# Feed-forward operand places queued by hand, GLA state in pairs, norms behind the last sums

## The chip, the cores and the metric

One core of one Trainium2 chip. The metric is device microseconds of one execution of the whole program, the median of several runs. TensorE is PE, VectorE DVE, ScalarE ACT, GpSimd POOL, and SP is the queue that issues the transfers.

## What is computed

One decoder layer, x of 1024 tokens by 1024 columns, float32. The parts that the change touches:

```python
# gated linear attention, per chunk of tokens (scan over chunks, 4 heads, 64 x 128 state a head)
def step(state, xs):
    qn, kn, vn, dn = xs
    o = jnp.einsum('bhid,bhde->bhie', qn, state)
    state = state * dn[..., None] + jnp.einsum('bhjd,bhje->bhde', kn, vn)
    return state, o
...
# feed-forward
h = rmsnorm(x, pre_ffn_g[l])
gt = causal_dwconv(h @ w_ff_gate[l], ff_conv_w[l]) + ff_conv_b[l]
y = (jax.nn.gelu(gt, approximate=True) * (h @ w_ff_up[l])) @ w_ff_down[l]
x = x + rmsnorm(y, post_ffn_g[l])
```

Besides these the layer has the input projection, a short convolution, dilated attention, gates and an output projection.

## The kernel before

**Products.** A float32 matrix is split into a high and a low part (`split`, L155 to L159: ACT copies the high part, L158, and DVE subtracts it, L159), and each product is three matmuls, high by high, high by low, low by high. Dense products are done two by two blocks at a time with seven products instead of eight. `seven` (L265 to L320) takes 256 columns of a weight: it loads two raw halves (L169, 512 KB each), splits the operands 0, 1, 5, 6 from them, lets POOL form the combined ones (L279, L281, L283, L285), and issues the products 0 to 5, of 12 matmuls of 128x512 each (L292 to L295), with sums between them:

- L302 (ACT) and L304 (DVE): the first block of the result, from the banks X (product 0) and Y (1);
- L307 (ACT): from Z, product 2;
- L310 (ACT) and L313 (DVE): from X, product 3, and from Z, product 4;
- L315 (DVE): from X, product 5.

Product 6 is put off: `last_product` issues it behind product 0 of the next `seven`. It goes on in the bank X of its own block, so it has to wait for L315 of that block. Operands 0 to 3 lie in one slot of the pool `wp` and 4 to 6 in the other; a slot is free again when the last product that reads it has ended.

**Feed-forward, first stage** (L1320 to L1365). Ten chunks of 256 columns follow one done beforehand. Each has a `seven` on the gate's weight (a gate block), whose results go through the convolution (`conv`, L1270 to L1284: ACT L1278, DVE L1279, L1280, L1282, L1283, ACT L1284), and one on the up weight (an up block), whose results are multiplied on (L1342). `forms` (L1291 to L1307) then stores the result's blocks to DRAM and lets POOL make four combined ones (`made`, L1295), stored as well (`keep`, L1287), in the order 5, 7, 6, 3. The first of them overwrites a22 and so waits for a22's store.

**Feed-forward, second stage** (L1443 to L1497). Again seven products, in the order 2, 1, 5, 6, 3, 7, 4, each over 11 chunks, in four groups of matmuls of 128x512 (L1469), with sums L1475 to L1484. The operands of a step are loaded, combined and split some steps ahead. The table `ENDS` says behind which step the norm of which tile comes: `h` is `finish_half` (squares L1423, multiplication L1425) and `f` is `finish` (the reciprocal root and L1440). Product 7's sums (L1484) were issued with high priority.

**GLA state loop** (L797 to L826). Eight chunks of 128 tokens. For each head one product of the chunk itself (L805, 128 deep) and one with the state (L807, 64 deep: two heads share the partitions) add up in one place of a bank; the next state's update is a product with 64 columns of weights per head (L812), and DVE scales and adds (L817). Results leave by ACT (L823) and DVE (L826). Matmuls of the branch projection (`p`, L198 to L202) are put between the chunks by the scheduler, and behind the loop follow a norm (L836), POOL's L838 and transposes (L842).

Where no order is written out, a scheduler sets each engine's queue; every engine works off its own in order.

## Time and profile before

| what | us |
|---|---|
| median of 3 runs | 1990.79 |
| lowest, highest | 1985.05, 1993.75 |
| the profiled execution | 1983.94 |
| its span | 1982.1 |
| PE, DVE, ACT, POOL busy | 1897.9, 1302.5, 875.7, 756.7 |

The granted clock of PE is 0.987 of full speed in the mean. A row of a timeline gives start, duration, engine, line, operation and tiles; matmuls are pipelined, so a row's duration is longer than the distance from one start to the next. The GLA state loop lies at 937 to 975 us of the span, the feed-forward's first stage at 1360 to 1758, its second behind it.

### The profile page before, as it was taken

How to read it: one execution, taken by the hardware profiler on the slowest of the kernel's cores; microseconds unless marked ns; L12 is line 12 of the kernel's file. 1: busy time of each engine (PE TensorE's matmuls, PEld its weight loads, DVE VectorE, ACT ScalarE, POOL GpSimd, SP SyncE). 2: the span in 40 equal slices, each digit the busy share in tenths (PEclk: the TensorE clock that was granted, in tenths of full speed). 3: DMA queues.
4: the chain of work that ended last, by engine and by line, in shares of the span. 5: the costliest groups of instructions: out<-in, count | busy, mean ns of one | idle time of the engine just before them, and what ended most of it. 6: DMA issues, size and time to landing. Idle time of an engine off the chain costs nothing.

```text
span 1982.1 us, 26264 instructions
## 1 busy us (share of the span) xinstructions
PE 1897.9 (96%) x9705; PEld 1601.8 (81%) x9705; DVE 1302.5 (66%) x1913; ACT 875.7 (44%) x1618; POOL 756.7 (38%) x457
## 2 busy tenths in 40 slices
PE   6999999999999999999999898998999999999997
PEld 5988778888787999899688776886888788878885
DVE  8755665677777332578545577577667766678595
ACT  5343345454444323435356623343434443454543
POOL 4522334554555221102214463016444444516172
PEclk9999999999999999999999998999999999999998
DMA  4121323232323424113467554221323233378752
GB/s 174 64 91 59 122 85 122 92 126 91 122 96 126 135 75 146 59 38 102 137 194 218 168 173 157 85 101 54 106 87 127 80 107 105 108 279 319 264 179 101
DMA packets 187072, 251.53 MB, mean 127 GB/s; under 512 B 30017, under 2 KB 121023, under 8 KB 186944
## 3 DMA queue, kind: packets, MB, share of 16 engines
q1 hardware_dynamic: 186944, 249.86, 37.5%
q8 instruction: 76, 1.25, 0.2%
q14 instruction: 52, 0.43, 0.1%
HBM read 183.34 MB, written 66.47 MB: 126 GB/s over the span
## 4 chain that ended last, share of the span: by engine, by line
PE 64%; DVE 18%; issue 5%; POOL 4%; ACT 4%; DMA 4%; SPq 0%; DVEq 0%; POOLq 0%; ACTq 0%
PE sX L295 19%; PE sZ L295 8%; DVE wl L159 6%; PE sY L295 5%; PE fY L1469 4%; PE fX L1469 4%; PE vX L567 3%; PE vZ L567 2%; PE mx L1229 1%; PE mx L1230 1%; PE mx L1228 1%; PE gs L749 1%; ACT wh L158 1%; PE p L198 1%; PE p L200 1%
## 5 line engine op out<-in xcount | busy, mean ns | idle before, releaser
L159 DVE TENSOR_TENSOR wl<-raw,wh 128x512 fp32r<-128x512 f32 (+1 forms) x214 | 216.1, 1043 | 119.7 <-ACT wh L158 116.7
L295 PE MATMUL sX<-T,wh 128*128 128x512 f32 x720 | 224.3, 393 | 10.5 <-DVE ring L315 9.8
L158 ACT ACTIVATE wh<-raw 128x512 fp32r<-128x512 f32 (+1 forms) x226 | 146.1, 670 | 78.6 <-PE sX L295 59.6
L295 PEld LDWEIGHTS sX<-T,wh 128*128 128x128 f32 x720 | 134.8, 189 | 42.8 <-DVE ring L315 14.0
L295 PE MATMUL sX<-FT,wh 128*128 128x512 f32 x480 | 149.3, 392 | 9.1 <-DVE ring L315 6.8
L295 PE MATMUL sX<-T,wl 128*128 128x512 f32 x360 | 140.7, 391 | 0.0
L506 POOL TENSOR_TENSOR fr<-fr 128x512 f32<-128x512 f32 x48 | 71.8, 1496 | 144.0 <-ACT fr L499 142.6
L295 PEld LDWEIGHTS sX<-FT,wh 128*128 128x128 f32 x480 | 89.2, 188 | 32.2 <-DVE ring L315 11.5
L159 DVE TENSOR_TENSOR wl<-fr,wh 128x512 fp32r<-128x512 f32 x90 | 67.7, 773 | 64.8 <-ACT wh L158 64.1
L158 ACT ACTIVATE wh<-fr 128x512 fp32r<-128x512 f32 (+1 forms) x97 | 61.8, 657 | 77.0 <-PE sX L295 48.4
L295 PE MATMUL sX<-FT,wl 128*128 128x512 f32 x240 | 93.5, 389 | 0.0
L1295 POOL TENSOR_TENSOR fb<-fb 128x512 f32<-128x512 f32 x40 | 56.9, 1423 | 91.6 <-DMA d_fa<-fb 89.9
L279 POOL TENSOR_TENSOR fr<-raw 128x512 f32<-128x512 f32 x30 | 40.8, 1360 | 122.2 <-DMA raw<-in_w_gate_dram 45.7
L159 DVE TENSOR_TENSOR ops<-rw,ops 128x512 fp32r<-128x512 f32 x72 | 64.6, 927 | 28.4 <-ACT ops L158 28.2
L295 PEld LDWEIGHTS sX<-T,wl 128*128 128x128 f32 x360 | 68.0, 189 | 14.5
L285 POOL TENSOR_TENSOR raw<-raw 128x512 f32<-128x512 f32 x50 | 79.5, 1590 | 0.0
L507 DVE TENSOR_TENSOR ring<-ring,fr 128x512 f32<-128x512 f32 x48 | 57.2, 1193 | 30.8 <-POOL fr L506 29.3
L295 PE MATMUL sZ<-T,wh 128*128 128x512 f32 x240 | 73.9, 389 | 0.0
L1469 PE MATMUL fX<-ops 128*128 128x512 f32 x312 | 73.8, 391 | 0.0
L302 ACT ACTIVATE ring<-sX 128x512 f32<-128x512 f32 x48 | 28.5, 594 | 95.9 <-PE sX L295 75.2
L1469 PEld LDWEIGHTS fX<-ops 128*128 128x128 f32 x312 | 59.0, 189 | 12.3
L283 POOL TENSOR_TENSOR fr<-raw,fr 128x512 f32<-128x512 f32 x30 | 49.8, 1661 | 46.4 <-DVE wl L159 46.4
(552 smaller groups left out, 5623.2 us busy)
## 6 DMA issues: line engine op xcount, KB each, us to landing
rw<-in_w_ff_down_dram SPq DMA_DIRECT2D x99, 256.0 KB
raw<-in_w_in_dram SPq DMA_DIRECT2D x48, 512.0 KB
rw<-d_fa SPq DMA_DIRECT2D x77, 256.0 KB
d_fa<-fb SPq DMA_DIRECT2D x70, 256.0 KB
raw<-in_w_gate_dram SPq DMA_DIRECT2D x24, 512.0 KB
d_sig<-ring SPq DMA_DIRECT2D x48, 256.0 KB
d_qk<-ring SPq DMA_DIRECT2D x48, 256.0 KB
raw<-in_w_ff_gate_dram SPq DMA_DIRECT2D x22, 512.0 KB
```

The source lines that it names most:

```text
L158: S.activation(h, src, AF.Copy)
L159: eng.tensor_tensor(l, src, h.bitcast(F32), op=OP.subtract)
L279: G.tensor_tensor(s1, A21, A22, op=OP.add)
L283: G.tensor_tensor(s1, A12, s2, op=OP.subtract)
L285: G.tensor_tensor(A21, A11, A21, op=OP.subtract)
L295: PE.matmul(ps, a[x][:, k], b[y][:, k], start=first and k == 0 and n == 0, stop=k == 3 and n == 2, skip_group_check=not first)
L302: S.activation(c11, X, AF.Copy)
L506: G.tensor_tensor(sw, sw, sin[:, hs], op=OP.mult)
L507: V.tensor_tensor(as_(o), as_(o), perm(sw), op=OP.add)
L567: PE.matmul(o, b[y][:, k, ts], a[:, x, k], start=first and t % 2 == 0 and k == 0 and n == 0, stop=k == 3 and n == 2, skip_group_check=not ...
L1295: G.tensor_tensor(o, p, q, op=op)
L1469: PE.matmul(P[t], o[:, a, ts], o[:, b], start=st, stop=c + k == NCH - 1 and x == 2, skip_group_check=i not in (2, 1, 5))
```

## The change

- In the feed-forward's first stage a block's seven operands take seven of eight single places in turn, instead of two slots. Their splits are issued behind given sums of the block before (`issue_after`): operands 0 and 1 behind sums 2 and 1, operands 2 and 3 behind sums 3 and 4, the others behind 3 and 5, on ACT and DVE. Other uses of `seven` stay as they were.
- `forms` makes its four in the order 7, 5, 6, 3, with 7 written over a11.
- The GLA state holds two heads side by side, 256 columns, with zeros where they don't meet. A state product is one of 128 deep and 256 columns for two heads, and so is the update; the update's scaling on DVE is four instructions of 64x128 instead of two of 128x128.
- In the second stage the norms come later (`ENDS`); what they issue on DVE once product 7's sums are out is queued behind the last of these, and the high priority is gone.

```diff
--- before.py
+++ after.py
@@ -270,21 +270,33 @@
         r0, r1 = wload([v[:, :4, c0:c0 + 256], v[:, 4:, c0:c0 + 256]], [8, 256])
         A11, A21, A12, A22 = r0[:, :, :128], r0[:, :, 128:], r1[:, :, :128], r1[:, :, 128:]
         s1, s2 = [t.rearrange("p (k c) -> p k c", k=4) for t in tmp]
-        sets = []
-        for i in range(2):
-            sets.append([wp.tile([128, 4, 4, 128], F32R, name=n, tag=n) for n in ("wh", "wl")])
-        op = lambda i: (sets[i // 4][0][:, i % 4], sets[i // 4][1][:, i % 4])
-        split(*op(0), A11)
-        split(*op(1), A12)
+        if sops:
+            ops = [sops[0]() for i in range(7)]
+        else:
+            sets = [[wp.tile([128, 4, 4, 128], F32R, name=n, tag=n) for n in ("wh", "wl")] for i in range(2)]
+            ops = [(sets[i // 4][0][:, i % 4], sets[i // 4][1][:, i % 4]) for i in range(7)]
+        op = lambda i: ops[i]
+
+        def made(i, src):
+            with ExitStack() as es:
+                if sops:
+
+                    for k in ((2, 1) if i < 2 else (3, 4) if i < 4 else (3, 5)):
+                        if k in sums_taken:
+                            es.enter_context(tc.issue_after(sums_taken[k].ins))
+                split(*op(i), src)
+
+        made(0, A11)
+        made(1, A12)
         G.tensor_tensor(s1, A21, A22, op=OP.add)
-        split(*op(2), s1)
+        made(2, s1)
         G.tensor_tensor(s2, s1, A11, op=OP.subtract)
-        split(*op(3), s2)
+        made(3, s2)
         G.tensor_tensor(s1, A12, s2, op=OP.subtract)
-        split(*op(4), s1)
+        made(4, s1)
         G.tensor_tensor(A21, A11, A21, op=OP.subtract)
-        split(*op(5), A21)
-        split(*op(6), A22)
+        made(5, A21)
+        made(6, A22)
 
         blk = lambda j, l: (B[l][0][:, 4 * j:4 * j + 4], B[l][1][:, 4 * j:4 * j + 4])
         tt = lambda i: (Ts[i][:, 0], Ts[i][:, 1])
@@ -301,18 +313,18 @@
         c11 = dst(0, 0)
         S.activation(c11, X, AF.Copy)
         prod(Y, op(1), blk(1, 0), True)
-        V.tensor_tensor(c11, c11, Y, op=OP.add)
+        sums_taken[1] = V.tensor_tensor(c11, c11, Y, op=OP.add)
         prod(Z, op(2), tt(0), True)
         c22 = dst(1, 1)
-        S.activation(c22, Z, AF.Copy)
+        sums_taken[2] = S.activation(c22, Z, AF.Copy)
         prod(X, op(3), tt(1), False)
         c12 = dst(0, 1)
-        S.activation(c12, X, AF.Copy)
+        sums_taken[3] = S.activation(c12, X, AF.Copy)
         use(0, 0, c11)
         prod(Z, op(4), blk(1, 1), False)
-        V.tensor_tensor(c12, c12, Z, op=OP.add)
+        sums_taken[4] = V.tensor_tensor(c12, c12, Z, op=OP.add)
         prod(X, op(5), tt(2), False)
-        V.tensor_tensor(c22, c22, X, op=OP.add)
+        sums_taken[5] = V.tensor_tensor(c22, c22, X, op=OP.add)
         use(0, 1, c12)
         use(1, 1, c22)
 
@@ -323,6 +335,13 @@
 
 
     pending = []
+
+    sops, sums_taken = [], {}
+
+    def op_places():
+
+        ts = [[wp.tile([128, 4, 4, 128], F32R, name=n, tag=n) for n in ("wh", "wl")] for i in range(2)]
+        return Ring([(h[:, i], l[:, i]) for h, l in ts for i in range(4)])
 
     def last_product():
         while pending:
@@ -795,35 +814,40 @@
                              PQ[:, 2 + a, (2 * bp + bb) * 128:(2 * bp + bb) * 128 + 128], ident)
         ins = S.activation(kin[:, 2 * bp:2 * bp + 2], p.rearrange("p (b c) -> p b c", c=256), AF.Copy)
     ssg = sm.tile([128, 32], F32, name="ssg", bufs=1)
+
+
     state = None
-    states = slot("t2", [128, 2, 2, 128], name="states")
+    states = slot("t2", [128, 2, 2, 256], name="states")
+    G.memset(states, 0.0)
     for b in range(8):
-        po = [pt(tag, "go")[:, :256].rearrange("p (a e) -> p a e", a=2) for tag in "ot"]
-        for h in range(4):
-            bs = slice((h % 2) * 64, (h % 2) * 64 + 64)
-            p = po[h % 2][:, h // 2]
-            PE.matmul(p, Sb[:, b, h], gv[:, b, h * 128:h * 128 + 128], start=True, stop=b == 0)
+        po = [pt(tag, "go")[:, :256] for tag in "ot"]
+        for a in range(2):
             if b:
-                PE.matmul(p, qk[bs, h // 2, b * 128:b * 128 + 128], state[bs, h // 2], start=False, stop=True)
+                PE.matmul(po[a], qk[:, a, b * 128:b * 128 + 128], state[:, a], start=True, stop=True)
+            for w in range(2):
+                h = 2 * a + w
+                PE.matmul(po[a][:, w * 128:w * 128 + 128], Sb[:, b, h], gv[:, b, h * 128:h * 128 + 128],
+                          start=not b and w == 0, stop=True, skip_group_check=b > 0 or w == 1)
         if b < 7:
-            p2 = pt("s", "gst")[:, :256].rearrange("p (a e) -> p a e", a=2)
-            for h in range(4):
-                bs = slice((h % 2) * 64, (h % 2) * 64 + 64)
-                PE.matmul(p2[bs, h // 2], kin[:, b, h * 64:h * 64 + 64], gv[:, b, h * 128:h * 128 + 128],
-                          start=True, stop=True)
+            p2 = pt("s", "gst").rearrange("p (a e) -> p a e", a=2)
+            for a in range(2):
+                PE.matmul(p2[:, a], kin[:, b, a * 128:a * 128 + 128], gv[:, b, a * 256:a * 256 + 256],
+                          start=a == 0, stop=True, skip_group_check=a == 1)
             new = states[:, b % 2]
             for a in range(2):
-                if b:
-                    V.scalar_tensor_tensor(new[:, a], state[:, a], dec[:, a, b:b + 1], p2[:, a],
-                                           op0=OP.mult, op1=OP.add)
-                else:
-                    V.tensor_copy(new[:, a], p2[:, a])
+                for w in range(2):
+                    bs, es = slice(w * 64, w * 64 + 64), slice(w * 128, w * 128 + 128)
+                    if b:
+                        V.scalar_tensor_tensor(new[bs, a, es], state[bs, a, es], dec[bs, a, b:b + 1], p2[bs, a, es],
+                                               op0=OP.mult, op1=OP.add)
+                    else:
+                        V.tensor_copy(new[bs, a, es], p2[bs, a, es])
             state = new
         for h in range(4):
-            S.activation(gv[:, b, h * 128:h * 128 + 128], po[h % 2][:, h // 2], AF.Square,
+            S.activation(gv[:, b, h * 128:h * 128 + 128], po[h // 2][:, h % 2 * 128:h % 2 * 128 + 128], AF.Square,
                          accum_out=ssg[:, 4 * b + h:4 * b + h + 1])
-        for w in range(2):
-            V.tensor_copy(gv[:, b].rearrange("p (a w e) -> p a w e", w=2, e=128)[:, :, w], po[w])
+        for a in range(2):
+            V.tensor_copy(gv[:, b, a * 256:a * 256 + 256], po[a])
     rg = rstd(ssg, 128, 32)
 
 
@@ -1301,10 +1325,10 @@
             keep(c, 4, a22)
         if il == (1, 0):
             keep(c, 2, a12)
-            made(5, a22, a21, a22, OP.add)
-            made(7, a21, a11, a21)
-            made(6, a11, a22, a11)
-            made(3, a12, a12, a11)
+            made(7, a11, a11, a21)
+            made(5, a21, a21, a22, OP.add)
+            made(6, a22, a22, a11)
+            made(3, a12, a12, a22)
 
 
     first = [wcols(w_fg2, 0), wcols(w_fu2, 0)]
@@ -1325,6 +1349,8 @@
     for il in ((0, 0), (1, 1), (1, 0)):
         forms(0, ys, il)
 
+    sops.append(op_places())
+    sums_taken.clear()
     ring = halves_ring(("t2", "t0", "t1"))
     yring = Ring([fb[:, i] for i in (0, 1, 3)])
     STMP = [fb[:, 2, :512], fb[:, 2, 512:]]
@@ -1444,7 +1470,8 @@
 
     ALONE = {5 * NCH + 8: 3, 6 * NCH: 3, 6 * NCH + 6: 5}
 
-    ENDS = {(7, 1): "h0", (7, 3): "f0 h1", (7, 5): "f1 h2", (7, 7): "h3", (4, 3): "f2 h4 h5", (4, 4): "f3 h6", (4, 5): "h7"}
+    ENDS = {(7, 1): "h0", (7, 4): "f0", (4, 0): "h1 h2", (4, 3): "f1 h3 f2 h4", (4, 4): "f3 h5 h6", (4, 5): "h7"}
+    taken = None
     ready = []
     X = [pt("g", "fX") for t in range(4)]
     Y = [pt(tag, "fY") for tag in ("s", "s", "t", "o")]
@@ -1480,19 +1507,19 @@
                 elif i == 3:
                     V.tensor_tensor(C12[:, t], C12[:, t], P[t], op=OP.add)
                 elif i == 7:
-                    with tc.high_priority():
-                        V.tensor_tensor(C22[:, t], C22[:, t], P[t], op=OP.add)
+                    taken = V.tensor_tensor(C22[:, t], C22[:, t], P[t], op=OP.add)
                 else:
                     finish_half(4 + t, P[t], 0)
                     finish(4 + t)
-        for what in ENDS.get((i, c), "").split():
-            t = int(what[1])
-            if what[0] == "h":
-                if t < 4:
-                    finish_half(t, C11[:, t], 0)
-                finish_half(t, (C12, C22)[t // 4][:, t % 4], 1)
-            else:
-                finish(t)
+        with tc.issue_after(taken.ins) if taken else nullcontext():
+            for what in ENDS.get((i, c), "").split():
+                t = int(what[1])
+                if what[0] == "h":
+                    if t < 4:
+                        finish_half(t, C11[:, t], 0)
+                    finish_half(t, (C12, C22)[t // 4][:, t % 4], 1)
+                else:
+                    finish(t)
         n += w
```

DVE's queue in a gate block; L304, L313 and L315 are the sums, `wl` the low parts of operands, `fb` and `raw` their sources. Before:

```order
L304 TENSOR_TENSOR ring<-ring,sY 128x512
L1279 SCALAR_TENSOR_TENSOR fb<-ring,cols,fb 128x511
L1280 SCALAR_TENSOR_TENSOR fb<-ring,cols,fb 128x510
L159 TENSOR_TENSOR wl<-raw,wh 128x512 x2
L159 TENSOR_TENSOR wl<-fb,wh 128x512 x2
L313 TENSOR_TENSOR ring<-ring,sZ 128x512
L1279 SCALAR_TENSOR_TENSOR fb<-ring,cols,fb 128x511
L1282 SCALAR_TENSOR_TENSOR fb<-ring,cols,fb 128x1
L315 TENSOR_TENSOR ring<-ring,sX 128x512
L1280 SCALAR_TENSOR_TENSOR fb<-ring,cols,fb 128x510
```

and in the changed kernel, where the lines are 12 (sums) or 24 (convolution) further down, L316, L325 and L327 being the sums:

```order
L316 TENSOR_TENSOR ring<-ring,sY 128x512
L1303 SCALAR_TENSOR_TENSOR fb<-ring,cols,fb 128x511
L1304 SCALAR_TENSOR_TENSOR fb<-ring,cols,fb 128x510
L159 TENSOR_TENSOR wl<-raw,wh 128x512 x2
L325 TENSOR_TENSOR ring<-ring,sZ 128x512
L159 TENSOR_TENSOR wl<-fb,wh 128x512 x2
L1303 SCALAR_TENSOR_TENSOR fb<-ring,cols,fb 128x511
L1306 SCALAR_TENSOR_TENSOR fb<-ring,cols,fb 128x1
L1304 SCALAR_TENSOR_TENSOR fb<-ring,cols,fb 128x510
L327 TENSOR_TENSOR ring<-ring,sX 128x512
L1307 SCALAR_TENSOR_TENSOR fb<-ring,cols,fb 128x2
```

Two splits have moved behind the sum of product 4, and the sum of product 5 has moved behind one more instruction of the convolution.

DVE's queue up to product 7's sums (L1484) in the second stage, with the numbers of the buffers; `rr`, `rt` and `ro` belong to norms. Before:

```order
L151 TENSOR_SCALAR rt_14914<-rt_14914 128x1
L153 TENSOR_TENSOR ro_14917<-rr_14912,rt_14914 128x1
L1440 SCALAR_TENSOR_TENSOR acc_13392<-acc_13392,ro_14917,x1r_13394 128x512 x2
L159 TENSOR_TENSOR ops_13382<-rw_13380,ops_13382 128x512
L159 TENSOR_TENSOR ops_13382<-bs_13389,ops_13382 128x512
L159 TENSOR_TENSOR ops_13383<-rw_13380,ops_13383 128x512
L159 TENSOR_TENSOR ops_13383<-bs_13389,ops_13383 128x512
L1484 TENSOR_TENSOR acc_13393<-acc_13393,fX_13396 128x512
```

and in the changed kernel, where these sums are L1510:

```order
L159 TENSOR_TENSOR ops_13293<-rw_13291,ops_13293 128x512
L159 TENSOR_TENSOR ops_13293<-bs_13300,ops_13293 128x512
L159 TENSOR_TENSOR ops_13294<-rw_13291,ops_13294 128x512
L159 TENSOR_TENSOR ops_13294<-bs_13300,ops_13294 128x512
L1510 TENSOR_TENSOR acc_13304<-acc_13304,fX_13307 128x512
L1510 TENSOR_TENSOR acc_13304<-acc_13304,fX_13308 128x512
```

The norms have gone from between the splits; only splits stand ahead of the first of these sums.

PE's queue at one chunk of the GLA loop. Before (L812 the state's update, `p` the other matmuls):

```order
L812 MATMUL gst_7388<-gv_6095,gqk_6004 64x128 x3
L202 MATMUL p11_7576<-yH1h_7212,wh_7231 128x512
L198 MATMUL p10_7609<-yH1h_7212,wl_7232 128x512
L812 MATMUL gst_7411<-gv_6095,gqk_6004 64x128
L805 MATMUL go_7355<-gv_6095,Sb_6098 128x128
L807 MATMUL go_7355<-states_7266,gqk_6004 128x128
L805 MATMUL go_7356<-gv_6095,Sb_6098 128x128
L807 MATMUL go_7356<-states_7266,gqk_6004 128x128
```

and in the changed kernel (L826 the state products, L829 the chunk's own, L834 the update):

```order
L834 MATMUL gst_7358<-gv_6095,gqk_6004 128x256 x2
L826 MATMUL go_7329<-states_7266,gqk_6004 128x256
L829 MATMUL go_7329<-gv_6095,Sb_6098 128x128 x2
L826 MATMUL go_7330<-states_7266,gqk_6004 128x256
L829 MATMUL go_7330<-gv_6095,Sb_6098 128x128 x2
L834 MATMUL gst_7379<-gv_6095,gqk_6004 128x256 x2
```

Four state products have become two, the update's four two, and no `p` stands between.

## Rows read from the trace of the kernel before

**Rows 1.** The page, part 1: engine, busy us (share of the span), instructions.
```profile
PE 1897.9 (96%) x9705; PEld 1601.8 (81%) x9705; DVE 1302.5 (66%) x1913; ACT 875.7 (44%) x1618; POOL 756.7 (38%) x457
```

**Rows 2.** Waits, PE, 1360 to 1760: us in total, times, longest.
```profile
PE sX L295 <- DVE ring L315: 6.8, 11, 1.7
...
PE sX L295 <- ACT ring L310: 2.3, 1, 2.3
```

**Rows 3.** Timeline, PE, a gate block: start, duration, instruction, [idle before, releaser].
```profile
1457.24 0.62 PE L295 MATMUL sX<-FT,wh 128*128 128x512 f32 x2
...
1462.46 0.39 PE L295 MATMUL sX<-F0h,wl 128*128 128x512 f32 x1
1464.06 0.73 PE L295 MATMUL sX<-FT,wh 128*128 128x512 f32 x2 [1.21 <-DVE ring L315]
```

**Rows 4.** Timeline, DVE, the same gate block.
```profile
1458.76 2.37 DVE L159 TENSOR_TENSOR wl<-fb,wh 128x512 fp32r<-128x512 f32 x2
1461.06 0.67 DVE L313 TENSOR_TENSOR ring<-ring,sZ 128x512 f32<-128x512 f32 x1
1462.53 0.75 DVE L1279 SCALAR_TENSOR_TENSOR fb<-ring,cols,fb 128x511 f32<-128x511 f32 x1 [0.79 <-ACT fb L1278]
...
1463.32 0.68 DVE L315 TENSOR_TENSOR ring<-ring,sX 128x512 f32<-128x512 f32 x1
```

**Rows 5.** Chain of waits, 1440 to 1480: start, duration, what.
```profile
1451.30 4.30 DMA raw<-in_w_ff_gate_dram
...
1464.06 3.02 PE sX L295 x12
```

**Rows 6.** Timeline, PE, one chunk of the GLA state loop.
```profile
953.72 0.49 PE L805 MATMUL go<-gv,Sb 128*128 128x128 f32 x2
954.13 0.48 PE L807 MATMUL go<-states,gqk 64*128 64x128 f32 x2
```

**Rows 7.** Chain of waits, 925 to 994.
```profile
937.55 0.89 PE go L805 x8
...
952.40 0.59 PE gst L812 x8
```

**Rows 8.** Stretches: us, PE, PEld, DVE, ACT, POOL busy, PEclk, DMA, GB/s.
```profile
1900.00:1942.00 42.00, 36.29 (x161) 29.71 (x159) 41.64 (x62) 19.73 (x43) 25.27 (x16) 0.99 0.51 176
1942.00:1948.00 6.00, 5.95 (x14) 4.72 (x15) 5.07 (x7) 5.90 (x14) 3.77 (x3) 0.50 0.05 22
1942.00:1982.00 40.00, 32.93 (x132) 26.71 (x132) 20.07 (x44) 12.98 (x31) 10.07 (x7) 0.88 0.15 56
```

**Rows 9.** Timeline, PE, end stage.
```profile
1942.05 1.62 PE L1469 MATMUL fX<-wh 128*128 128x512 f32 x3 [5.76 <-DVE acc L1484]
```

**Rows 10.** Timeline, DVE, end stage.
```profile
1928.85 0.75 DVE L1440 SCALAR_TENSOR_TENSOR acc<-acc,ro,x1r 128x512 f32<-128x512 f32 x1
...
1930.72 1.78 DVE L1440 SCALAR_TENSOR_TENSOR acc<-acc,ro,x1r 128x512 f32<-128x512 f32 x1
...
1934.18 1.41 DVE L1440 SCALAR_TENSOR_TENSOR acc<-acc,ro,x1r 128x512 f32<-128x512 f32 x2
...
1937.49 1.42 DVE L1440 SCALAR_TENSOR_TENSOR acc<-acc,ro,x1r 128x512 f32<-128x512 f32 x2
...
1941.23 1.88 DVE L1484 TENSOR_TENSOR acc<-acc,fX 128x512 f32<-128x512 f32 x3
```

**Rows 11.** Line L921: duration ns min/median/max, first and last start, forms.
```profile
L921 PE MATMUL ds<-dA x128: 270/379/615, 997.2 to 1121.7; 128*128 128x256 f32 x88, 128*128 128x128 f32 x40
```

**Rows 12.** Groups of instructions, 925 to 976: busy us, mean ns, idle before.
```profile
L826 DVE COPY gv<-go 128x256 f32<-128x256 f32 x15 | 6.0, 421 | 6.8 <-ACT gv L823 6.8
...
L817 DVE SCALAR_TENSOR_TENSOR states<-states,dec,gst 128x128 f32<-128x128 f32 x12 | 4.1, 345 | 13.9 <-PE go L807 11.4 <-PE gst L812 2.5
```

**Rows 13.** Timeline, PE, behind the GLA loop.
```profile
984.39 0.66 PE L842 MATMUL yT<-cst,sg 128*128 128x128 f32 x4 [1.01 <-POOL sg L838]
```

**Rows 14.** Tile raw, 1400 to 1700: duration ns min/median/max.
```profile
L159 DVE TENSOR_TENSOR wl<-raw,wh x60: 677/693/1776, 1409.3 to 1690.1; 128x512 fp32r<-128x512 f32 x60
```

## The prediction

> **What bounds the kernel now.** I read the page first: TensorE (PE) is busy 96% of the span [rows 1]. So a change pays only where PE stands still or where its own instructions get cheaper, and PE's waits by stage, the timelines and the chain have to say where. Three places are touched.
>
> In the feed-forward's first stage PE waits 11 times, 6.8 us in all, for the sum L315 on VectorE (DVE), and once 2.3 us for the copy L310 on ScalarE (ACT) [rows 2]. One gate block shows the first kind. Product 5 starts at 1457.24; with the next block's product 0 behind it, 24 matmuls, 0.227 us apart, it reaches to 1462.7. The deferred seventh product needs product 5's bank and starts only at 1464.06, after 1.21 us idle [rows 3]. DVE's rows say why: L313, which needs only product 4 (done when product 5 starts), begins at 1461.06, since splits stand ahead of it, two of them of 2.37 us together; L1279 then waits for ACT, and L315 begins at 1463.32 [rows 4]. Twelve matmuls after such a restart take 3.02 us [rows 5] instead of 12 x 0.227 = 2.72.
>
> In the GLA state loop PE never stops; the price of an instruction is the limit. An intra-chunk product (128 rows deep) and a state product (64 rows deep) alternate, two instructions each, and a pair of instructions starts 0.41 us after the one before: 0.21 an instruction [rows 6]. Eight intra-chunk ones on end, in chunk 0, take 0.89, so 0.11 each; eight of the state update, with weights of 64 columns, 0.59, so 0.07 [rows 7].
>
> Before the last product of the end stage DVE is the bound: busy 41.64 of the 42 us up to 1942 [rows 8]. PE waits 5.76 us, up to 1942.05, for the sums L1484 [rows 9], the first of which starts at 1941.23 [rows 10]. From 1942 to 1948 the granted clock is 0.50, the lower of its two levels (1.2 GHz) [rows 8].
>
> **The change part by part.** *Operand places and forms.* A block's operands 2 and 3 get places of their own, so their splits needn't stand ahead of L313; in a gate block they are queued behind it, and L315 now behind both L1279 and L1280. Counted from the block's start (six products of 2.72 before 1457.24): product 4 ends at 16.3, L313 starts at 16.4 to 17.1 (a raw split may still run) and takes 0.67, mostly in the shadow of the next start; the two splits take 2.37; from L1279's start to L315's are 0.79 now, to which L1280 adds 0.75 at most; L315 takes 0.68 [rows 4]. With L313 at its full 0.67 that ends between 21.7 and 22.4; rows that follow each other start up to 0.1 before the last has ended, five times here, so 21.2 to 21.9. PE needs it at 16.32 + 2 x 2.72 = 21.76. I leave 0.1 us of stall per chunk. The present loss: 6.8 less the last block's 1.7, which has no gate block behind it, is 5.1 [rows 2], and ten slow restarts of 0.3 make 3.0; of 8.1, 1.0 stays. On GpSimd (POOL) the forms now begin with one that doesn't wait for a store, stores follow earlier, and I let the first block's L310 wait 0.4 instead of 2.3: 1.9 more. Of the 9.0 I take **8**, as a late L310 also puts off the first L315. Ends: 10, and 1.9 where the gates gain nothing. No instruction is added; but on ACT both raw splits now stand ahead of L310, and on SP the weight loads lie between the stores 7, 5, 6, 3 (rival (d)).
>
> *GLA.* Before, a chunk with state: eight pairs at 0.41 to 0.42, 3.3 us, and the update 0.59 for eight: over seven chunks 27.4 [rows 6, 7]. After: 8 intra-chunk instructions at 0.11, and 4 of the state and 4 of the update with 256 columns. The nearest row for those is L921: 88 of its 128 matmuls have 256 columns and the median lasts 379 ns, the shortest, of 128 columns, 270 [rows 11]; 0.11 more than 0.11 is 0.22. So 0.89 + 0.88 + 0.88 = 2.65 us, 18.5 over seven: 9 us less. The memset on POOL is over before the loop. But hardly any other matmul now stands between the chunks, so what DVE needs must fit: four updates of 345 ns and two copies of 421 make 2.2 us [rows 12]. 0.4 is to spare, and I give back 0.3 a chunk: **7**. Ends: nothing (a stall of 1.3 us per chunk, three such DVE steps), and 10, as the matmuls moved behind the loop can cover idle time there, such as 1.01 us for L838 [rows 13].
>
> Against this part stands a rule. Row and column pieces of 64 run as independent tiles in parallel, up to twice as fast, says the Trainium skill, TensorEngine Tiling (Array Packing), Theoretical Speedup; a change of mode drains the engine, says its Key Properties. By the first alone, half-filled arrays gain nothing in the state products and lose in the update: the loop would get 2 us longer (0.29 for each chunk's update), and the sum would be 14.7 instead of 23.7. The trace bears out both: 0.07 against 0.11 for narrow weights, which I have charged, and 0.21 for alternating depths, twice the 0.11.
>
> *End stage.* The norms of tiles f1 to f3 leave DVE's queue ahead of L1484. Their six L1440 take 0.75 + 1.78 + 1.41 + 1.42 us, 5.4, and their small steps come on top [rows 10]. The first L1484 then starts by 1935.9, before PE is ready at 1936.3 (1942.05 less 5.76), and the pause goes: 5.8. Without it I expect no fall of the clock; 6 us at half speed are nearly 3 more. Together **8.7**. The norms go beside product 4, where DVE is busy 20.07 of 40 us [rows 8]; the chain behind the last matmul stays. Ends: 9, and 3 (the clock alone, or half the wait).
>
> **Sum.** 7 + 8 + 8.7 = 23.7 us off the profiled execution's 1983.94 gives 1960.2. That execution stands 0.35% under the median of the runs, 1990.79, so the forecast is **1967 us**. About 0.5% (10 us) can be told from no change.
>
> **Rivals.**
> (a) The gates keep their stalls. L315 stands behind two splits and L1280, and POOL works at the same time: a raw split lasts 0.69 us in the median and 1.78 at worst [rows 14]. If both last 1.78, 1.2 more than 2.37, L315 ends up to 1.3 late, as now. Only 1.9 is won in the stage: 1973. (A VectorE instruction with two SBUF inputs and a GpSimd one that reads SBUF exclude each other for their whole length: the Trainium skill, SBUF — State Buffer, SBUF: two separate sides. 1.78 against 0.69 agrees.)
> (b) GLA gains nothing, because update, state product and a bank's turn-around become a chain with nothing between: 1974. For it: the other matmuls go. Against it: 0.4 us to spare, and the update is queued a chunk ahead of its use. The rule of independent tiles alone would come out here too, at 1976. With (a) as well, 1980 to 1982.
> (c) The change doesn't do what it says in the end stage: another wait takes the place of L1484's, such as product 4's last operand late behind the norms. 3 us are won there: 1973.
> (d) Slower: a weight load lands late. ACT splits both raw operands ahead of L310, and L310 must be done 16.3 us into a block; about 0.6 each for the last split and the copy set the second landing's limit at 15.1. The load whose landing is on the chain now takes 4.30 us from 1451.30, so lands 14.7 into the block [rows 5]. From 0.4 us later on PE waits; as long as L310's 2.3 in the first block [rows 2], and in all twenty blocks, that is 46 us. Less the other gains that is 22 to 30 more than now: 2013 to 2021. Against it: the forms don't wait first any more, so what the loads queue behind starts earlier.
> (e) None of it tells: the new order waits for the same things in all three places, 1985 to 1992.
>
> **Chances.** Forecast 0.57; (a) 0.15; (b) 0.07; both 0.03; (c) 0.05; (d) 0.07; (e) 0.06. Faster (under 1981): the forecast, (a), (b), (c), and half of the pair, 0.855, of which I move 0.075 to the same, since many prices here are borrowed from other places: 0.78. Same: that, (e) and the other half, 0.14. Slower: (d) and a little of (e), 0.08. The range: down, all upper ends (10 + 10 + 9 = 29 us off, 1962 at the median) and the 0.25% by which runs scatter, 1957; up, over (a), (b), (c) and half of the pair, 1981. Left out are (d), (e) and half the pair, some 0.15, and a little of the forecast.
>
> **What would show it.** Right: PE's wait for L315 in the stage falls from 6.8 us to under 3, the last block's with it, and that for L310 under 0.5; the GLA loop's products and updates are 7 us shorter with gaps under 0.5; L1484 starts before PE is ready, and the clock after it stays at the upper level. Wrong: ten waits for L315 near 0.8 with splits of 1.7 ahead (a); gaps before the state products (b); a wait for operands in product 4 (c); waits for L310 or a split in many blocks (d).

## The result, and the profile after

The changed kernel takes 1967.6 us in the median of four runs (1962.24 to 1971.89), the kernel before 1987.92 in the median of four beside it; the ratio is 0.9896, with a 95% interval of 0.987 to 0.9923. Run again beside the last three experiments it came to 0.9916 (0.9898 to 0.9934). The forecast was 1967. The profiled execution is the slowest of the four, 1971.89 us.

The lines of the changed kernel lie further down: the sums L302, L304, L307, L310, L313 and L315 are now L314, L316, L319, L322, L325 and L327, the convolution's L1279, L1280 and L1282 are L1303, L1304 and L1306, and L1484 is L1510.

On the page of the profile PE's share has not moved [rows 1]:

```profile
PE 1891.7 (96%) x9649; PEld 1601.9 (81%) x9649; DVE 1317.8 (67%) x1927; ACT 876.2 (44%) x1618; POOL 761.4 (39%) x458
```

**The first feed-forward stage.** PE's waits there answer to [rows 2]:

```profile
PE sX L307 <- DVE ring L327: 4.1, 2, 2.6
...
PE sX L307 <- ACT ring L322: 1.4, 1, 1.4
```

Two waits for product 5's sum are left where there were eleven, but the two, in the first gate block and the last up block, have grown from 2.7 us together to 4.1. The short ones are now seen at the weight loads (PEld), which run ahead of the matmuls. Weight loads between the first block and the last, before:

```profile
PEld sX L295 <- DVE ring L315: 7.9, 9, 1.6
```

and after:

```profile
PEld sX L307 <- DVE ring L327: 3.6, 9, 0.5
```

So the nine gate blocks between, called steady here, still wait, 0.4 us each instead of 0.9; in seven of them the sum comes too late for PE, by 0.13 to 0.20 us, in two 0.11 and 0.15 us early. A late one, in DVE's timeline (answers to [rows 4]):

```profile
1570.90 0.67 DVE L325 TENSOR_TENSOR ring<-ring,sZ 128x512 f32<-128x512 f32 x1
1571.49 1.28 DVE L159 TENSOR_TENSOR wl<-fb,wh 128x512 fp32r<-128x512 f32 x2
1572.70 1.77 DVE L1303 SCALAR_TENSOR_TENSOR fb<-ring,cols,fb 128x511 f32<-128x511 f32 x1
...
1574.52 0.74 DVE L1304 SCALAR_TENSOR_TENSOR fb<-ring,cols,fb 128x510 f32<-128x510 f32 x1
1575.18 0.68 DVE L327 TENSOR_TENSOR ring<-ring,sX 128x512 f32<-128x512 f32 x1
```

POOL's row in the same block:

```profile
1572.32 1.60 POOL L295 TENSOR_TENSOR fb<-raw,fb 128x512 f32<-128x512 f32 x1 [1.89 <-DVE wl L159]
```

and PE's (answers to [rows 3]):

```profile
1575.50 0.39 PE L307 MATMUL sX<-F0h,wl 128*128 128x512 f32 x1
1575.91 0.74 PE L307 MATMUL sX<-FT,wh 128*128 128x512 f32 x2
```

L325 starts 16.9 us into the block, 3.2 earlier than before, and both splits take 1.28, not 2.37. Then L1303, beside POOL's L295, takes 1.77 us instead of 0.75, L1304 follows, and L327 ends at 1575.86, 0.13 behind 1575.73, when the last matmul of product 0 has had its 0.227 us. The first two matmuls after it are 0.34 us apart instead of 0.227.

In the first block PE still waits for the copy of product 3, L322 (L310 before), 1.4 us instead of 2.3, but for another reason. Before, ACT ran L310 after 2.52 us idle, which a store ended:

```profile
1378.44 0.60 ACT L310 ACTIVATE ring<-sX 128x512 f32<-128x512 f32 x1 [2.52 <-DMA d_fa<-fy]
```

Now the convolution's last step, L1308, waits in ACT's queue for DVE's L1304, and both raw splits and L322 stand behind it:

```profile
1374.84 0.73 ACT L1308 ACTIVATE fb<-fb,cols 128x512 f32<-128x512 f32 x1 [2.19 <-DVE fb L1304]
1375.47 1.13 ACT L158 ACTIVATE wh<-raw 128x512 fp32r<-128x512 f32 x2
1376.51 0.58 ACT L322 ACTIVATE ring<-sX 128x512 f32<-128x512 f32 x1
```

The last up block waits longer than before, when it was 1.67:

```profile
1750.50 0.73 PE L307 MATMUL sX<-FT,wh 128*128 128x512 f32 x2 [2.57 <-DVE ring L327]
```

DVE's rows ahead of it:

```profile
1745.09 0.69 DVE L159 TENSOR_TENSOR wh<-rw,wh 128x512 fp32r<-128x512 f32 x1 [1.02 <-ACT wh L158]
1745.70 0.68 DVE L325 TENSOR_TENSOR ring<-ring,sZ 128x512 f32<-128x512 f32 x1
...
1746.90 0.68 DVE L1368 TENSOR_TENSOR fb<-fb,ring 128x512 f32<-128x512 f32 x1
1747.50 2.35 DVE L159 TENSOR_TENSOR wl<-rw,wl 128x512 fp32r<-128x512 f32 x2
1749.78 0.67 DVE L327 TENSOR_TENSOR ring<-ring,sX 128x512 f32<-128x512 f32 x1
```

The splits belong to the second stage's operands; L325 and L327 stand between them; L1368 is the multiplication for block (0,1). Behind this wait the granted clock falls, which it did not in the trace of before (stretches: us, busy times as in [rows 8], PEclk, DMA share, GB/s):

```profile
1750.00:1754.00 4.00, 3.50 (x11) 2.82 (x12) 1.83 (x3) 0.63 (x1) 1.28 (x1) 0.73 0.84 313
1754.00:1758.00 4.00, 4.00 (x17) 3.22 (x16) 3.05 (x4) 3.48 (x7) 1.78 (x1) 0.85 0.64 216
```

**GLA.** A chunk (answers to [rows 6]), and PE's waits from the loop to the transposes:

```profile
961.69 0.59 PE L826 MATMUL go<-states,gqk 128*128 128x256 f32 x2
962.12 0.61 PE L829 MATMUL go<-gv,Sb 128*128 128x128 f32 x4
962.56 0.60 PE L826 MATMUL go<-states,gqk 128*128 128x256 f32 x2
...
963.36 0.48 PE L198 MATMUL p<-yH1h,wh 128*128 128x512 f32 x1
```

```profile
PE yT L866 <- POOL sg L862: 3.9, 3, 1.8
PE gst L834 <- DVE states L844: 0.2, 1, 0.2
```

Two state products and four of the chunk's own take 1.67 us where eight pairs took 3.3: two instructions of 256 columns start 0.43 us before the next row, four of 128 columns 0.44, which are the 0.22 and 0.11 an instruction that were forecast. In the whole loop one wait for DVE is left, of 0.2 us. Behind it PE waits 3.9 us for POOL's L862 (before: L838, 2.0).

**End stage.** DVE (answers to [rows 10]), and the stretch around product 7's end (answers to [rows 8]):

```profile
1930.81 0.68 DVE L159 TENSOR_TENSOR ops<-bs,ops 128x512 fp32r<-128x512 f32 x1
1931.41 1.87 DVE L1510 TENSOR_TENSOR acc<-acc,fX 128x512 f32<-128x512 f32 x3
```

```profile
1931.00:1937.00 6.00, 6.00 (x28) 4.95 (x27) 5.82 (x9) 3.85 (x8) 1.30 (x1) 1.00 0.00 0
```

The first L1510 comes right behind the last split, PE has no idle time, and the granted clock stays at the upper level (1.00, which is 2.4 GHz).

In every trace three lengths can be read from first and last starts of PE's lines: *GLA*, from the first transpose of kT (L794) to the first score (L921); *FF*, from the first product sZ of the feed-forward to the first fX of its second stage; *end*, from the last fY to the last fX.

| us | GLA | FF | end | ratio of times (95%) |
|---|---|---|---|---|
| before | 58.0 | 418.0 | 68.6 | 1 |
| changed kernel | 51.6 | 416.4 | 59.8 | 0.9896 (0.987 to 0.9923) |
| e1 GLA alone | 52.5 | 418.4 | 66.6 | 0.9964 (0.9952 to 0.9975) |
| e2 places and forms alone | 58.5 | 416.8 | 66.6 | 0.9975 (0.9966 to 0.9984) |
| e3 norms alone | 58.5 | 423.6 | 60.2 | 0.9964 (0.9954 to 0.9975) |
| e4 sum 5 first, and last block | 52.5 | 407.3 | 59.9 | 0.9866 (0.9853 to 0.9878) |
| e6 places alone | 58.5 | 413.6 | 68.8 | 0.9942 (0.9926 to 0.9959) |
| e7 forms alone | 58.0 | 410.3 | 67.1 | 0.9934 (0.9918 to 0.995) |
| e8 sum 5 first | 51.6 | 407.9 | 59.8 | 0.9844 (0.9825 to 0.9863) |
| e9 GLA grouped alone | 48.9 | 420.3 | 66.9 | 0.9931 (0.9914 to 0.9948) |
| e10 changed, no places | 52.5 | 409.3 | 59.9 | 0.9892 (0.9874 to 0.9911) |
| e11 e8 with e9 | 47.8 | 408.5 | 59.9 | 0.9847 (0.9825 to 0.9869) |
| e12 changed, again | 52.7 | 416.5 | 59.8 | 0.9916 (0.9898 to 0.9934) |

Profiled executions of one code differ by some us in stages that no edit touches, since short stretches of half clock come and go (the changed kernel's was 5.2 us behind at 798 us already, before any of the three places); the columns leave those stages out. FF itself holds 3.4 us of half clock in the traces of the changed kernel, e2, e6, e9 and e12, some 7 in that of e3, and none in the others.

FF can be taken apart further. The up blocks between the first block and the last take 19.04 us each from their first product sY to the next block's, and so does a gate block in which PE doesn't wait. FF is 18 such lengths (342.7 us), what the nine steady gate blocks take beyond that, and the two ends: the first block, from FF's start to the next block's first sY, and the last up block, from its first sY to the end of FF.

| us | first block | nine gate blocks, beyond 19.04 each | last up block |
|---|---|---|---|
| before | 20.3 | 6.9 | 48.2 |
| before, e1, e3, e9 (all with its code there) | 19.6 to 21.6, mean 20.4 | 6.9 to 10.3, mean 8.3 | 47.2 to 50.5, mean 48.6 |
| changed kernel | 20.3 | 2.6 | 50.7 |
| changed kernel, e2, e12 | 20.3 to 21.7, mean 21.2 | 1.6 to 2.6, mean 2.0 | 50.5 to 50.7, mean 50.6 |
| e6 places alone | 21.6 | 1.6 | 47.6 |
| e7 forms alone | 19.4 | 0 | 48.2 |
| e10 changed, no places | 18.9 | 0 | 47.7 |
| e4, e8, e11 sum 5 first | 18.1 to 18.2 | 0 | 46.4 to 47.7 |

### The profile page after: what moved, and what is told of

Its sections match the earlier page's. It is cut to its first block, busy times and chain, and to the rows that moved or that the text cites. A ratio compares the mean times of both kernels' runs of the same rounds, so it can differ in the third digit from the quotient of the medians.

```text
span 1970.1 us, 26193 instructions
## 1 busy us (share of the span) xinstructions
PE 1891.7 (96%) x9649; PEld 1601.9 (81%) x9649; DVE 1317.8 (67%) x1927; ACT 876.2 (44%) x1618; POOL 761.4 (39%) x458
## 4 chain that ended last, share of the span: by engine, by line
PE 70%; DVE 14%; issue 5%; POOL 4%; ACT 4%; DMA 3%; SPq 0%; DVEq 0%; ACTq 0%; POOLq 0%
PE sX L307 21%; PE sZ L307 10%; PE sY L307 6%; PE fX L1496 6%; PE fY L1496 4%; PE vX L586 4%; DVE wl L159 3%; PE vZ L586 2%; PE mx L1253 1%; PE mx L1254 1%; PE mx L1252 1%; PE gs L768 1%; PE p L198 1%; POOL fr L525 1%; PE p L200 1%
## 5 line engine op out<-in xcount | busy, mean ns | idle before, releaser
L307 PE MATMUL sX<-T,wh 128*128 128x512 f32 x720 | 227.1, 397 | 10.9 <-DVE ring L327 10.2
L307 PEld LDWEIGHTS sX<-T,wh 128*128 128x128 f32 x720 | 136.7, 191 | 44.0 <-DVE ring L327 14.4
L307 PE MATMUL sX<-FT,wh 128*128 128x512 f32 x480 | 150.1, 394 | 5.9 <-DVE ring L327 4.1
L307 PE MATMUL sX<-T,wl 128*128 128x512 f32 x360 | 142.1, 395 | 0.0
L307 PEld LDWEIGHTS sX<-FT,wh 128*128 128x128 f32 x480 | 89.7, 189 | 28.6 <-DVE ring L327 8.6
L307 PE MATMUL sX<-FT,wl 128*128 128x512 f32 x240 | 94.1, 392 | 0.0
L307 PEld LDWEIGHTS sX<-T,wl 128*128 128x128 f32 x360 | 68.8, 191 | 14.8
L1319 POOL TENSOR_TENSOR fb<-fb 128x512 f32<-128x512 f32 x40 | 61.7, 1543 | 42.4 <-DVE fb L1368 33.9
L307 PE MATMUL sZ<-T,wh 128*128 128x512 f32 x240 | 73.9, 389 | 0.0
L158 ACT ACTIVATE ops<-rw 128x512 fp32r<-128x512 f32 x72 | 43.2, 626 | 55.5 <-PE fX L1496 23.3
L295 POOL TENSOR_TENSOR fr<-raw,fr 128x512 f32<-128x512 f32 x30 | 49.7, 1656 | 46.5 <-DVE wl L159 46.5
```

What stands on the lines that cost most here:

```text
L158: S.activation(h, src, AF.Copy)
L295: G.tensor_tensor(s1, A12, s2, op=OP.subtract)
L307: PE.matmul(ps, a[x][:, k], b[y][:, k], start=first and k == 0 and n == 0, stop=k == 3 and n == 2, skip_group_check=not first)
L1319: G.tensor_tensor(o, p, q, op=op)
```

## The experiments

**e1, e2, e3: each part alone.** Each is the kernel before with one of the change's parts:

```diff
# e1: the GLA loop, nothing else
-    states = slot("t2", [128, 2, 2, 128], name="states")
+    states = slot("t2", [128, 2, 2, 256], name="states")
+    G.memset(states, 0.0)
...
# e2: the places, their queueing, and the forms, nothing else
+    sops.append(op_places())
+    sums_taken.clear()
...
# e3: ENDS, the queueing behind the sums, nothing else
+    ENDS = {(7, 1): "h0", (7, 4): "f0", (4, 0): "h1 h2", (4, 3): "f1 h3 f2 h4", (4, 4): "f3 h5 h6", (4, 5): "h7"}
```

> Only the GLA state in pairs is taken over. If the loop's instructions are what was paid for, from the end of the branch loop (L712, 850 us) to the first scores (L921) the trace is 6 to 7 us shorter than before and the time 5 to 8 us lower (ratio 0.996 to 0.9975). If the gain needs what follows behind the loop (or is lost in it, as rule of independent tiles has it), the time is the same within 2 us and the first L921 stands where it stood.

> Only the feed-forward's operand places and the order of the forms. As the profile of the changed kernel reads (steady gate blocks 0.43 us better each, the last up block 0.9 us and its clock worse, the first block mixed), the stage is 1 to 3 us shorter and the time 1 to 4 us lower. As predicted, it would be 8 us lower. If the stage's gain is what makes the timed runs better than the profiled one, it is 5 us lower or more.

> Only the place of the norms in the last stage. If the wait of 5.8 us and the half clock behind it are one thing, both go: 8 to 9 us lower (ratio 0.9955 to 0.996), and no stretch of clock 0.50 near 1942. If the fall of the clock has another cause, 6 us lower and the clock still falls within product 4.

Measured beside 28 runs of the kernel before (median 1986.53): e1 1979.92, e2 1980.98, e3 1979.09. That is 7.2, 5.0 and 7.2 us off by the ratios, 19.3 together, and the whole change measured 20.7 at first and 16.7 (13.1 to 20.3) when run again: within the noise the parts add up. e1's time came as expected. From the end of the branch loop its trace is 3.2 us shorter instead of 6 to 7, with a stretch of 10 us at half clock in it that before lacks; its GLA length, behind that stretch, is 5.4 shorter. e3's 7.2 (5.0 to 9.1) lies under the 8 to 9 expected, and no stretch of half clock is left before its last matmul. e2 lies at the edge of both of its expectations: its trace is only 1.2 us shorter in the stage than the one of before, its runs 5 us.

e2 still has the old end stage, and with it the wait, 4.8 us long where it was 5.8 before:

```profile
PE fX L1492 <- DVE acc L1507: 4.8, 1, 4.8
```

**e4, e8: the sum of product 5 ahead of the convolution.** e8 is the changed kernel with the first edit, e4 has both:

```diff
-        use(0, 1, c12)
+        with tc.issue_after(sums_taken[5].ins) if sops else nullcontext():
+            use(0, 1, c12)
...
# e4 alone, in the second stage's operands
-        split(o[:, 0], o[:, 1], a)
-        split(o[:, 2], o[:, 3], b)
+        with tc.issue_after(sums_taken[5].ins) if i == 2 and 4 <= c < 8 else nullcontext():
+            split(o[:, 0], o[:, 1], a)
+            split(o[:, 2], o[:, 3], b)
```

> The changed kernel, with the convolution of block (0,1) queued behind the sum of product 5 on DVE, and the splits of four second-stage operands queued behind the last block's sum. If the 0.2 us waits in the gate blocks come from L1304 (the convolution's third instruction) ahead of the sum and the 2.57 us wait in the last up block from two splits ahead of it, all waits for L327 in the stage but the first vanish: stage 4 to 7 us shorter than the changed kernel's, time 4 to 7 us lower than its 1967.6. If DVE has no room for it, the splits of operands 4 to 6 come late and PE waits for L159 instead.

> The changed kernel with the convolution of block (0,1) behind product 5's sum, without the second edit of e4. If the waits of 0.2 us and the slow restarts behind them are what e4 won, 3 to 4 us of e4's gain over the changed kernel stay here and the last up block still waits 2.5 us for L327, with a stretch of half clock behind it. If e4's gain was the last block's, this runs as the changed kernel.

In a gate block `use(0, 1, c12)` issues the convolution of both blocks (0,0) and (0,1), so both move behind the sum on DVE; in an up block it issues the multiplication of block (0,1), which moves too.

e4 took 1958.71 us, e8 1957.64 (on another chip, where before was 1988.93). The FF length falls by 9.1 and 8.5 us against the changed kernel's 416.4, more than either expectation had; e4 has no wait for L327 left, and e8, without the edit for the last block, one, in that block:

```profile
PE sX L307 <- DVE ring L327: 0.5, 1, 0.5
```

So what is won comes from the order of the sum and what stood ahead of it, and most of it not in the steady gate blocks. They give 2.6 us, the first block 2.2 and the last up block 3.6 (e8 against the changed kernel). In the first block the waits for L322 (1.42) and L327 (1.55) are gone: L1308 no longer stands ahead of L322 on ACT. In the last up block the wait fell from 2.57 to 0.5, and the clock behind it doesn't fall:

```profile
1739.76 1.29 DVE L159 TENSOR_TENSOR wl<-rw,wl 128x512 fp32r<-128x512 f32 x2
1740.97 0.68 DVE L327 TENSOR_TENSOR ring<-ring,sX 128x512 f32<-128x512 f32 x1
1741.57 1.29 DVE L1369 TENSOR_TENSOR fb<-fb,ring 128x512 f32<-128x512 f32 x2
```

The multiplication (L1368, here L1369) has gone behind the sum, which is 0.6 us of it, and the two splits last 1.29 us instead of 2.35, 1.1 more; why they are shorter was not isolated. The second edit adds nothing that can be told.

**e6, e7: places and forms apart.** e6 is e2 with the forms in their old order; e7 is the kernel before with this alone:

```diff
-            made(5, a22, a21, a22, OP.add)
-            made(7, a21, a11, a21)
-            made(6, a11, a22, a11)
-            made(3, a12, a12, a11)
+            made(7, a11, a11, a21)
+            made(5, a21, a21, a22, OP.add)
+            made(6, a22, a22, a11)
+            made(3, a12, a12, a22)
```

> Of the feed-forward part only the operand places and the queueing; the forms in their old order 5, 7, 6, 3. If the gain of e2 (5 us) comes from the splits behind L313, all of it stays: 4 to 6 us lower than before. If POOL's early start is what lets the combined operands be ready in time, half of it goes, and the gate blocks wait for L327 by 0.5 us or more.

> Only the order of the forms. If it acts by itself, POOL's waits for stores (89.9 us) fall to under half, the first block's L310 waits 1.4 instead of 2.3, and the time is 1 to 2 us lower; the gate blocks' waits for L315 stay at 0.2 to 1.2. If POOL's earlier work collides with DVE's splits ahead of L313, these waits grow and the time is 2 us higher or more.

Both expectations were too low. e7 is 13.1 us faster than before by its ratio (9.9 to 16.3), e6 11.5 (8.2 to 14.7), both on the chip of e8, and both edits at once (e2) 5.0 (3.2 to 6.8) on another. The stage shows less than these runs but the same order: against the mean of four traces with the old code, 420.1 us, FF is 9.8 us shorter in e7, 6.5 in e6 and 3.5 in the mean of the changed kernel, e2 and e12. Where the rest of e6's and e7's gain lies was not found. Each alone clears the steady gate blocks or nearly: e7's PE waits for L315 in the stage are

```profile
PE sX L295 <- DVE ring L315: 3.0, 2, 1.7
```

(the first block and the last up block). e6 has one left in a steady gate block and one in the last up block, 1.1 us each, and a longer one for the copy in the first block:

```profile
PE sX L307 <- ACT ring L322: 2.7, 1, 2.7
PE sX L307 <- DVE ring L327: 2.2, 2, 1.1
```

In e7 POOL waits 37.4 us for stores (89.9 before):

```profile
POOL fb L1295 <- DMA d_fa<-fb: 37.4, 20, 2.9
```

and in a gate block DVE's queue has the order of before [rows 4], with its pieces shorter:

```profile
1461.22 1.28 DVE L159 TENSOR_TENSOR wl<-fb,wh 128x512 fp32r<-128x512 f32 x2
1462.42 0.67 DVE L313 TENSOR_TENSOR ring<-ring,sZ 128x512 f32<-128x512 f32 x1
1463.89 0.75 DVE L1279 SCALAR_TENSOR_TENSOR fb<-ring,cols,fb 128x511 f32<-128x511 f32 x1 [0.80 <-ACT fb L1278]
...
1464.69 0.68 DVE L315 TENSOR_TENSOR ring<-ring,sX 128x512 f32<-128x512 f32 x1
```

The two splits from `fb` last 1.28 us, not 2.37. POOL's L285, which ran beside them before, is over when they start; first before, then e7:

```profile
1458.25 1.74 POOL L285 TENSOR_TENSOR raw<-raw 128x512 f32<-128x512 f32 x1
1459.01 1.74 POOL L285 TENSOR_TENSOR raw<-raw 128x512 f32<-128x512 f32 x1
```

L315 stands ahead of L1280 and ends at 1465.37, 0.7 before PE comes to it at 1466.07; in the nine steady blocks it is 0.7 to 1.2 us early. With the places, L327 stands behind one more instruction: in e6 it is 0.2 us early in eight of the nine, in the traces of both edits between 0.2 early and 0.2 late.

**e10, e12: the changed kernel without the places, and again.**

```diff
-    sops.append(op_places())
-    sums_taken.clear()
```

> The changed kernel without the eight operand places (two slots again), everything else kept. If places and forms work against each other, as e2, e6 and e7 say (5 us together, 13 for the forms alone), this is 5 to 9 us faster than the changed kernel: 1959 to 1963, with no wait for L327 in the steady gate blocks. If e7's runs only fell well, it runs as the changed kernel or is slower.

> The changed kernel once more, on the chip of e9 to e11, so that they can be told from it: ratio to before 0.987 to 0.992, and in its profile the waits of 0.2 us in most of the gate blocks.

Without the places their queueing is gone too. On one chip, e10 took 1964.48 us (1960.51 to 1967.08), just over what was expected, and e12 1968.8 (1964.61 to 1972.39), as expected. The FF length is 409.3 against 416.5, near e7's 410.3; the waits for L327 in the stage are two, in the first and the last block, and none in a steady one:

```profile
PE sX L307 <- DVE ring L327: 2.4, 2, 1.3
```

So beside the new order of forms the places cost rather than win: by the traces 7 us, by the medians 4.3, with ratios whose intervals overlap (0.9874 to 0.9911 and 0.9898 to 0.9934). The stage is shown to be shorter; by how much the whole time is, the runs leave open.

**e5, e9, e11: the price of alternating.** e9 is the kernel before with the chunk's products of a GLA chunk first and its state products, 64 rows deep as before, behind them:

```diff
-            PE.matmul(p, Sb[:, b, h], gv[:, b, h * 128:h * 128 + 128], start=True, stop=b == 0)
+            PE.matmul(p, Sb[:, b, h], gv[:, b, h * 128:h * 128 + 128], start=h < 2, stop=True,
+                      skip_group_check=h > 1)
+        for h in range(4):
+            bs = slice((h % 2) * 64, (h % 2) * 64 + 64)
+            p = po[h % 2][:, h // 2]
             if b:
-                PE.matmul(p, qk[bs, h // 2, b * 128:b * 128 + 128], state[bs, h // 2], start=False, stop=True)
+                PE.matmul(p, qk[bs, h // 2, b * 128:b * 128 + 128], state[bs, h // 2], start=False, stop=True,
+                          skip_group_check=True)
```

> The kernel before, with the four chunk products of a GLA chunk issued first and the four state products (still 64 rows deep, no zeros) behind them. If the price of 0.21 an instruction is that of alternating between depths, a chunk's sixteen instructions take 1.8 us or less instead of 3.3, and from the first kT to the first L921 the trace is 6 to 10 us shorter than before's 58. If it is the price of a 64-row product as such, nothing changes. If the 64-row products of the two halves run in parallel, the eight state instructions take about 0.45 us together.

e5 had `start=True` in all four chunk products, so that the state's part doesn't add up in all places as the reference has it; its times are not used.

> As e5, with the first of the two chunk products of a bank alone starting it. If alternating between depths is what was paid for, the eight chunk instructions take 0.9 us, the eight state ones 0.9 or less, and from the first kT to the first L921 the trace is 8 to 12 us shorter than before's 58, more than the 6 that the pairs with zeros gave; the time is 7 to 11 us lower than before. If depth 64 itself costs 0.21, nothing changes.

> e8 with e9's GLA loop in place of the pairs. If both hold: 2 to 5 us under e8 (ratio to before 0.982 to 0.984). If the shorter loop only lengthens the wait behind it for POOL's L862, it runs as e8.

e9 took 1972.16 us beside 1986.68, 13.7 less by the ratio (10.3 to 17.1). A chunk on PE:

```profile
951.10 1.16 PE L805 MATMUL go<-gv,Sb 128*128 128x128 f32 x8
952.19 0.71 PE L811 MATMUL go<-states,gqk 64*128 64x128 f32 x8
952.83 0.43 PE L817 MATMUL gst<-gv,gqk 128*64 128x128 f32 x2
```

Eight instructions of the chunk take 1.09 us to the first state product and the eight state ones 0.64: 1.73, where the alternating pairs took 3.3 and the changed kernel's take 1.67. The state's update stays at 0.07 an instruction. The GLA length is 48.9, 9.1 less than before; the pairs with zeros gave 6.1 in the mean of six traces. That depth 64 itself is dear is thereby refuted: the same instructions, regrouped, are cheap. The runs won more than the 7 to 11 us expected and than the trace's 9.1; where the rest lies is open. e11, which has both this and e8's edit, took 1952.9 us on that chip, 15.9 less than the changed kernel beside it, the lowest time of all. By its ratio, 0.9847, it can't be told from e8's 0.9844 on another chip; that the two edits add up is seen in the trace alone, where GLA is 47.8 against 51.6. In its gate blocks L327 is ready before product 5 is and waits for PE:

```profile
1442.18 0.69 DVE L325 TENSOR_TENSOR ring<-ring,sZ 128x512 f32<-128x512 f32 x1 [1.06 <-PE sZ L307]
1442.78 1.28 DVE L159 TENSOR_TENSOR wl<-fb,wh 128x512 fp32r<-128x512 f32 x2
1444.83 0.69 DVE L327 TENSOR_TENSOR ring<-ring,sX 128x512 f32<-128x512 f32 x1 [0.76 <-PE sX L307]
1445.43 1.41 DVE L1306 SCALAR_TENSOR_TENSOR fb<-ring,cols,fb 128x511 f32<-128x511 f32 x2
```

## Why the prediction was right, and where it was not

**The sum.** 23.7 us were forecast, 20.7 measured and 16.7 when run again. That the time lies 0.6 us from the forecast is in part luck: the forecast started from a median before of 1990.79, which the fourth run took to 1987.92, 2.9 us lower, and that makes up for the 3.0 us by which the gain fell short. Two of three terms held; the third was sized too large.

**GLA: held, for partly another reason.** 7 forecast, 7.2 measured in e1, 6.1 in the traces. The price of alternation was read rightly: by e9's rows a chunk's sixteen instructions need 0.89 + 0.64 without it, and 3.3 - 1.5 over eight changes is 0.22 us a change of depth. The Trainium skill, TensorEngine Tiling (Array Packing), Key Properties, has it that a change of mode drains the engine. The trace agrees in so far as each change costs time; a drain as such is not seen in it. Narrow pieces are cheaper too, 0.08 and 0.07 us against 0.11. The 0.3 us a chunk that I gave back were not lost in the loop (0.2 in all); they went behind it, where PE waits 1.9 us longer for POOL's L862, and where, as the queues read, the matmuls taken out of the loop have still to run; what these cost there was not measured. The zeros themselves were not needed: grouping alone did more, as e9 shows.

**End stage: held, a little less.** 8.7 forecast, 7.2 measured in e3, 7.5 in the traces (67.4 in the mean of six with the old order, 59.9 in seven with the new). The wait goes whole, as worked out. It was 5.8 us in the profile that I read and 4.8 to 6.2 in the six; the fall of the clock behind it was 6.8 us long there, in e6 and in e7, and 3.4 in e1, e2 and e9. I had taken one execution's for all.

**First feed-forward stage: the step that failed.** "I leave 0.1 us of stall per chunk ... Of the 9.0 I take **8**." It was 5.0 in e2's runs, 3.5 in the traces (420.1 in the mean of four with the old code, 416.6 in three). The table of the three pieces says where the rest went.

The nine steady gate blocks did what was forecast, nearly: by the prediction's own terms they lost 6.7 us, of which 0.9 were to stay. They lost 6.9 in the trace of before and 8.3 in the mean of four; 2.6 and 2.0 are left. The way there was not the one worked out. L327 comes at 21.9 us into the block that is shown, against 21.76, because L1303 lasts 1.77 us beside POOL where I had 0.75; that it is no later is luck, since the two splits ahead of it lasted 1.28 where I had 2.37. This is rival (a)'s mechanism in another instruction. The first two matmuls of a restart are 0.11 us further apart even where PE hardly waits.

The first block was to give the other 3.2: 1.9 from L310, and its own share of the waits for L315. It gave nothing, 20.3 us before and after. The store that L310 had waited for is out of the way, but the gelu L1308 and both raw splits now stand ahead of it on ACT, so that PE waits 1.42 us and not 0.4, and the wait for product 5's sum grew from 1.07 to 1.55. The 2.3 that I started from was one execution's too: it is 1.5, 0.3 and 2.9 in e1, e3 and e9. The prediction had seen that both splits would stand there, and charged nothing for it.

The last up block I left out as having no gate block behind it, that is, at nothing. It got 2.5 us longer (2.0 in the means): it waits 2.57 us instead of 1.67, and the clock falls. Part of this is scatter, for with the old code it waits 0.64, 2.34 and 1.81 us in e1, e3 and e9, and in e3 the clock falls as well; the three new traces have 2.3 to 2.6. So two of the signs set for a right prediction didn't come: L310's wait under 0.5, and all waits for L315 under 3.

What I did not see at all: the two edits of this part work against each other. I gave the forms 1.9 us and the places the rest; alone, by their runs, the forms are worth 13 and the places 11.5, and both 5. In the steady gate blocks each alone empties the queue's jam: early forms let POOL be done before DVE's splits, and the places take two splits out of the way. With both, the sum stands behind L1304, beside POOL's L295, and the margin that the forms alone had is gone. But that is 2.0 of the 6.3 us by which FF is longer than with the forms alone; the rest lies in the first block and the last up block, 1.9 and 2.3 in the means. Of that one thing is seen: in e7 one raw split stands ahead of L310 on ACT and PE waits 0.91 us, with the places two stand there and it waits 1.42. The remainder was not isolated.

**The other rivals.** (b) did not come: 0.2 us of waits in the loop. (c) did not: PE has no wait in the last product. (d) did not as a whole: L322 is waited for once, in the first block, though by its mechanism, ACT's splits ahead of the copy. (e) did not.

## What to carry to other kernels

Price two edits to one queue apart and together: each may empty the same jam, and the second can then only cost. Price the first and the last turn of a loop apart from the steady ones, and from more than one trace. A sum that frees a bank for the next product belongs ahead of everything in its queue that PE does not wait for; one edit that put it there took another 8.5 us off the stage of the changed kernel. Where short and full-depth matmuls alternate, regroup them before padding them.

## What the runs showed of the hardware

A change between 128 and 64 rows of depth cost 0.22 us each time; 64-row matmuls of the two halves one behind the other took 0.08 us each, less than a full one's 0.11. After a wait of 2.3 to 2.6 us in the last up block the granted clock fell to its lower level (1.2 GHz), in the traces of the changed kernel, e2, e3 and e12; after 1.8 us or less there it stayed at the upper one (before, e1, e4, e6 to e11). Behind the longer wait of the old end stage the fall lasted 3.4 us in three traces and 6.8 in three others of the same code; the wait was 4.8 us in one of either kind (e2, e7).
